# Layer 0's attention: score products and transposes alternate, the projection goes in quarters, the out-projection's weights are fetched in one go

## The chip, the core and the metric

One core of a Trainium2 chip runs the whole program. The metric is the device time of one execution in microseconds (us), as the median of several runs. Beside it there is one execution taken by the hardware profiler. Engines are named as in the profile: PE (TensorE matmul), PEld (its weight load), DVE (VectorE), ACT (ScalarE), POOL (GpSimd), SP (the queue that issues the transfers).

## What is computed

A two-layer block of a transformer over 512 latent tokens and 256 context tokens, width 1024, in float32. Each layer is attention followed by a gated feed-forward network, both with a normalisation and a shift, scale and gate that come from a small conditioning vector. The change touches only the attention of layer 0, which is cut here to what matters:

```python
def _even_mixer(hx, hc, w_in, w_out, ...):      # hx: 512 tokens, hc: 256 tokens
    # 16 query heads of 64 in two groups, A (window, with sink) and B (dense); 4 query heads share one key/value head
    qa, ka, va, qb, kb, vb = split(h @ w_in)    # normalised per head, rotated for latent tokens
    # per head:  s = q k^T / 8 ;  p = softmax(s) ;  o = p v
    # A, latent: keys are the context and a window of 128 on both sides; B, latent: all 768 keys
    # context queries see the 256 context keys only
    out = concat(oa, ob) @ w_out
    x = x + gate * out
```

The four key/value heads give four batches of work, each with four query heads: batches 0 and 1 are A, 2 and 3 are B. The tokens are six tiles of 128: tiles 0 to 3 latent, 4 and 5 context.

## The kernel before

Every float32 product that needs the accuracy is done in two parts, a high and a low one (`hi = cast(x)`, `lo = x - hi`): the cast runs on ACT, the subtraction on DVE or POOL. The helper `unit` (L360 to L371) fetches a block of weights, casts it (L369) and subtracts (L370); its names are `wir`, `wih`, `wil` for the in-projection and `wor`, `woh`, `wol` for the out-projection.

**In-projection** (`in_proj0`, L499). For one batch and one token tile, 24 products `inps` (8 blocks of the contraction, three products each, L465 to L467) add up in one PSUM bank. ACT then copies the bank to `qkv` (L511); DVE rotates, POOL normalises, and the parts `qd` and `kd` are turned on PE (`qpt` L526, `kpt` L534) and copied by ACT to `qt` and `kT`. The turns wait in a list `due` and are taken from it one at a time while later products run. From batch 1 on there is one bank for `inps`.

**Attention** (`attend0`, L538). A step is one batch and one token tile; there are 24 steps in `steps`, in the order of tiles 4, 5, 0, 1, 2, 3 (in batch 3: 0 to 5). For each of its four heads a step forms the scores `sc` on PE (L569, plus mask products L571), then DVE takes the maximum (`mx` or `nm`, L578 to L582), ACT the exponential into `Pt` (L583), and after each pair of heads DVE a reciprocal `rc` (L592) and POOL the scaling of both heads' `Pt` (L595). Then `Pt` is turned by PE (`ppt`, L603, eight products for each two blocks of keys), copied back by ACT (L608) and DVE (L606), and multiplied with the values (`av`, L614). There are two buffers for `sc` and two PSUM banks that `ppt`, `qpt` and `kpt` share.

`scores0(i)` forms the scores of one head of step i, `transposes0(i-1)` turns two key blocks of the step before, `values0(i-1)` forms its `av`. Between them PE gets the next batch's projection in halves of 12 products (`half0`, counts in `HALVES`), and the modulation vectors of later parts (`mod_run`, products `mod` and `modcol`, raw data through a pool of two raw buffers that the weights share).

**What sets the order.** A scheduler orders every engine's instructions; but from the line `manual.__enter__()` on, PE keeps the order in which the program is written. Before the change that begins ahead of the first attention step. The written order of a step in batches 0 to 2 is:

```python
scores0(i); mod_ends(); scores0(i)
half0((n + 1) // 2)
transposes0(i - 1); scores0(i); transposes0(i - 1); scores0(i); transposes0(i - 1)
half0(n // 2)
values0(i - 1)
```

and in the first step of a batch (`elif i`) the four scores and the first two transposes run ahead of both halves. The weights of the next batch are fetched at the first step of a batch, all four units.

**Out-projection** (`OutProj`). Its eight weight units are made by `out_units` in batch 3, two at the end of step 18 (tile 0) and three each at steps 19 and 20, their subtractions turn by turn on POOL and DVE; each raw block waits for one of two raw buffers. The products `ops` (24 for one tile and one half of the width) begin at step 21.

Of the kernel before, what the change touches and what calls it, by code (L numbers as in the profile page):

```python
# [2 lines left out]

# [15 lines left out]
P = 128  # L19
# [43 lines left out]
def backbone(es: ExitStack, tc: tile.TileContext, x, c, ctx, c_ctx, mod_w, mod_b, norm_mix_w, norm_ffn_w,  # L63
# [418 lines left out]
    def weights0(b, wp, subs, new_tile=raw_tile):  # L482
# [3 lines left out]
        ws = []  # L486
        for u in range(4):
# [4 lines left out]
            ws.append(unit(wp, views, [P, 2, 384], WBUF, "wi", subs[u % len(subs)], new_tile))  # L492
        return ws
# [4 lines left out]
    def in_proj0(b, ws, tabs, wp, st, qp, later):  # L498

        wc, tb = tabs[b // 2]  # L500
# [4 lines left out]
        for t in CTX_FIRST:  # L505
            ps = acc_tile("inps", 384, one=0) if b or t in CTX_FIRST[-2:] else p_sc.pool.tile([P, 1024], F32, name="inps", tag="sc", bufs=2)[:, :384]
            project(ps, t, ws, 0, 384, range(4))
            yield
            project(ps, t, ws, 0, 384, range(4, KT))
# [3 lines left out]
            y, r = rotate(raw[:, 0:320], 4, 1, t, wc, tb, wp)  # L513
# [9 lines left out]
            def turn_q(t=t, qd=qd):  # L523
# [3 lines left out]
                qt = qp.tile([P, 4, P], F32R, name="qt", tag="qt", bufs=6)  # L527
# [611 lines left out]
    ws = weights0(0, wp.pool, (nc.vector,), start_tile)  # L1139
# [11 lines left out]
    due = []  # L1151

    proj = in_proj0(0, ws, tabs, wp.pool, even.pool, wp.pool, due)
    state = next(proj)
    for _ in range(2 * NT - 4):
        next(proj)
        if len(due) > 2:
            due.pop(0)()
    o_t = [keep.tile([P, KT, P], F32, name=f"o{t}", tag="xo", bufs=6) for t in range(NT)]
# [20 lines left out]
    def half0(n):  # L1180
        for _ in range(n):
            if len(due) > 2:
                due.pop(0)()
            next(proj, None)

# [11 lines left out]
    manual = tc.manual_schedule(engines={mybir.EngineType.PE})  # L1197
    manual.__enter__()
    HALVES = ((2, 2, 2, 4, 2, 4), (2, 2, 2, 2, 2, 2), (2, 2, 4, 2, 2, 0))
    RUNS = ((0, 0, 1, 1, 1, 0), (0, 1, 1, 1, 1, 1), (0, 0, 0, 1, 1, 1))  # L1200
    if True:
        for i, (b, t) in enumerate(steps):
            j = i % NT
            if j == 0 and b < 3:
                if b == 1:
                    tables0(1, tabs, wp.pool)
                ws = weights0(b + 1, wp.pool, (nc.gpsimd, nc.vector))
            if i == 0:
                for n in range(2):
                    scores0(i)  # L1210
                    scores0(i)
                    half0(1)
            if j == (0 if b else 2) and b < 3:
# [559 lines left out]
```

## Time and profile before

| | |
|---|---|
| median of 3 runs | 1728.89 us (1728.5 to 1729.42) |
| the profiled execution: its time | 1731.22 us |
| its span, first to last instruction | 1729.4 us, so 1.8 us lie around it |
| DVE busy | 1138.0 us, 66% |
| ACT busy | 940.6 us, 54% |
| POOL busy | 695.1 us, 40% |
| bytes read from HBM | 179.91 MB, 111 GB/s with what is written |

A row of the timeline gives the start, the time from the first start to the last end of the merged instructions, engine, line, operation and number; in brackets stands how long the engine sat idle just before it and what released it. The records of `inps` overlap, so that 12 of them lie about 2.1 us apart from start to start where each is shown with 0.34 us. The products `av`, `mod` and `modcol` show two records each. Granted clock is the share of the full TensorE clock that the throttle granted.

### The profile page before, as it was taken

To read this page: it belongs to the slowest core of one execution; us is meant where nothing else is said; L and a number is where in the kernel's file an instruction comes from. 1 tells how busy PE (TensorE), PEld (TensorE's weight loads), DVE (VectorE), ACT (ScalarE), POOL (GpSimd) and SP (SyncE) were. 2 spreads that over 40 slices of the span, in tenths; PEclk is the share of its full clock that TensorE was granted. 3 is DMA by queue.
4 is the path that set the end of the run, shared out by engine and by line. 5 is a ranking of instruction groups with operands and counts; after the bars stand their busy time and mean duration, and the time that the engine had idled before them with its cause. 6 is when DMAs were issued, how large, how long until landed. Compare 5 with 4: busy or idle time off the path is not lost. (4 is left out here: it accounts for less than half of the span.)

```text
span 1729.4 us, 28502 instructions
## 1 busy us (share of the span) xinstructions
PE 1647.4 (95%) x10378; PEld 1481.8 (86%) x10378; DVE 1138.0 (66%) x2009; ACT 940.6 (54%) x2010; POOL 695.1 (40%) x851
## 2 busy tenths in 40 slices
PE   6998989899999999999999899999997999999998
PEld 3877878677999999998777789999986899999887
DVE  3755646554798887767766655666666498887433
ACT  5555556644456655545554456666665465555321
POOL 1655545521345554412413366666643242222000
PEclk8899999999999999999999999999999999999999
DMA  9122221411365555439955311111103153332431
GB/s 315 51 68 67 95 65 50 158 49 50 99 185 164 156 158 167 136 109 342 303 171 163 107 45 62 53 41 44 46 13 122 31 143 103 105 106 58 137 94 69
DMA packets 217964, 194.64 MB, mean 113 GB/s; under 512 B 20000, under 2 KB 202592, under 8 KB 217824
## 3 DMA queue, kind: packets, MB, share of 16 engines
q1 hardware_dynamic: 217472, 192.62, 36.1%
q8 instruction: 81, 1.33, 0.3%
q14 instruction: 59, 0.48, 0.1%
q10 hardware_dynamic: 352, 0.21, 0.0%
HBM read 179.91 MB, written 12.87 MB: 111 GB/s over the span
## 5 line engine op out<-in xcount | busy, mean ns | idle before, releaser
L865 ACT CAST wbh<-wr 128x512 fp32r<-128x512 f32 x170 | 105.3, 621 | 145.5 <-PE p L897 76.5
L897 PE MATMUL p<-hT,wbh 128*128 128x256 f32 (+1 forms) x752 | 154.8, 299 | 0.0
L465 PE MATMUL inps<-wih,hT 128*128 128x384 f32 x384 | 136.7, 356 | 6.1 <-ACT qkv L668 6.0
L467 PE MATMUL inps<-wih,hT 128*128 128x384 f32 x384 | 130.4, 340 | 0.0
L466 PE MATMUL inps<-wil,hT 128*128 128x384 f32 x384 | 130.3, 339 | 0.0
L875 POOL TENSOR_TENSOR wbl<-wr,wbh 128x512 fp32r<-128x512 f32 x43 | 58.0, 1349 | 177.6 <-ACT wbh L865 177.6
L897 PEld LDWEIGHTS p<-hT,wbh 128*128 128x128 f32 x752 | 122.0, 191 | 0.2
L875 DVE TENSOR_TENSOR wbl<-wr,wbh 128x512 fp32r<-128x512 f32 x127 | 106.4, 844 | 22.4 <-ACT wbh L865 18.8
L897 PE MATMUL p<-hT,wbl 128*128 128x256 f32 (+1 forms) x376 | 112.1, 298 | 0.0
L897 PE MATMUL p<-t,wbh 128*128 128x384 f32 (+1 forms) x480 | 111.0, 317 | 0.0
L230 POOL TENSOR_TENSOR modp<-modp 128x512 f32<-128x512 f32 x40 | 57.5, 1439 | 119.1 <-ACT modp L229 119.1
L595 POOL TENSOR_SCALAR Pt<-Pt,rc 128x256 f32<-128x256 f32 (+3 forms) x96 | 74.0, 782 | 75.4 <-DVE rc L592 71.3
L897 PE MATMUL p<-hTt,wbh 128*128 128x256 f32 (+1 forms) x480 | 101.3, 303 | 0.0
L851 POOL TENSOR_TENSOR wr<-wr 128x512 f32<-128x512 f32 x40 | 61.1, 1528 | 88.4 <-DVE ws L856 87.4
L897 PE MATMUL p<-b,wbh 128*128 128x384 f32 x368 | 94.7, 339 | 0.2 <-DVE c L925 0.2
L865 ACT CAST wbh<-ws 128x512 fp32r<-128x512 f32 x120 | 69.5, 580 | 43.4 <-PE p L897 29.5
L370 POOL TENSOR_TENSOR wil<-wir,wih 128x768 fp32r<-128x768 f32 x38 | 71.2, 1874 | 48.6 <-ACT wih L369 48.1
L223 DVE SCALAR_TENSOR_TENSOR ma<-modw,cols,ma 128x256 f32<-128x256 f32 x140 | 85.5, 610 | 2.3
L897 PEld LDWEIGHTS p<-t,wbh 128*128 128x128 f32 x480 | 82.9, 189 | 0.0
L875 DVE TENSOR_TENSOR wbl<-ws,wbh 128x512 fp32r<-128x512 f32 x120 | 81.6, 680 | 1.7 <-ACT wbh L865 1.6
L897 PEld LDWEIGHTS p<-hTt,wbh 128*128 128x128 f32 x480 | 78.4, 191 | 3.1 <-ACT modp L229 2.1
L583 ACT ACTIVATE Pt<-sc,nm 128x256 f32<-128x256 f32 (+3 forms) x96 | 67.6, 706 | 24.6 <-DVE nm L579 15.1
(332 smaller groups left out, 5236.7 us busy)
## 6 DMA issues: line engine op xcount, KB each, us to landing
modw<-in_mod_w_dram SPq DMA_DIRECT2D x96, 512.0 KB, 4.6
wr<-in_ffn_w_in_dram SPq DMA_DIRECT2D x176, 256.0 KB, 3.2
wdr<-in_ffn_w_out_dram SPq DMA_DIRECT2D x66, 512.0 KB, 4.2
wir<-in_od_w_in_dram SPq DMA_DIRECT2D x96, 128.0 KB, 2.3
hidm<-hid SPq DMA_DIRECT2D x44, 192.0 KB, 3.9
hr<-hidm SPq DMA_DIRECT2D x22, 192.0 KB, 3.2
x<-in_x_dram SPq DMA_DIRECT2D x8, 512.0 KB, 8.7
wir<-in_ev_w_in_dram SPq DMA_DIRECT2D x16, 256.0 KB, 2.8
```

Source lines behind the costliest of these rows:

```text
L223: nc.vector.scalar_tensor_tensor(acc, w[:, k], scale[k], acc, ALU.mult, ALU.add)
L230: nc.gpsimd.tensor_add(pr[:, 0:2], pr[:, 0:2], pr[:, 2:4])
L370: (sub or nc.vector).tensor_sub(lo, raw, f32(hi))
L465: nc.tensor.matmul(ps, hs[0][:, k, :], a, start=k == 0, stop=False)
L466: nc.tensor.matmul(ps, hs[0][:, k, :], b, start=False, stop=False)
L467: nc.tensor.matmul(ps, hs[1][:, k, :], a, start=False, stop=k == KT - 1)
L583: turn["exp"] = nc.scalar.activation(p[:, :n], s, AF.Exp, bias=nm[:, c1], accum_out=sm[:, c1])
L595: nc.gpsimd.tensor_scalar(p[:, :n], p[:, :n], rc[:, hh:hh + 1], 1.0, ALU.mult, ALU.mult)
L851: nc.gpsimd.tensor_sub(w, raw[f, "G1"], w)
L865: nc.scalar.copy(hi, w)
L875: (nc.gpsimd if name == "G2" else nc.vector).tensor_sub(lo, raw[need[n]], f32(hi))
L897: nc.tensor.matmul(ps, w[:, k, :], H[b][h][:, k, :], start=first and k == 0 and q == 0, stop=final and k == 3 and q == 2, skip_group_check ...
```

## The change

The PE order of batches 0 to 3 is written anew, and four things around it change.

1. The whole projection of batch 0 is issued before the first attention step (before: 8 of its 12 halves). The first five steps are no longer held to the written order: PE's order there is the scheduler's.
2. The projection goes in quarters of 6 products, `quarters`; a turn from `due` is taken within each pair. In a step of batches 0 to 2 scores and transposes alternate, with a pair of quarters in the middle and one near the end. Every step has the same form, the first one of a batch too. The projection of the next batch starts at its first step in batch 0 as well (before: at the third).
3. Two of a batch's four weight units are fetched two steps ahead of the batch (`j == 4`), with six buffers for each of `wih` and `wil` in place of five.
4. In batch 3 the scores and transposes alternate in the same way.
5. The out-projection's raw weights are fetched by eight transfers in a row into a ring of sixteen blocks and the two raw buffers (`out_units0`); all eight subtractions are on DVE. One unit is made at step 18, two at 19, three at 20, two at 21. In batch 3, and for the first half of tile 3 behind it, the product with the gate goes to a buffer in SBUF and no longer back into PSUM.

```diff
-    for _ in range(2 * NT - 4):
-        next(proj)
...
+    for _ in range(2 * NT):
+        quarters(2)
+        turned0()
...
-    HALVES = ((2, 2, 2, 4, 2, 4), (2, 2, 2, 2, 2, 2), (2, 2, 4, 2, 2, 0))
-    RUNS = ((0, 0, 1, 1, 1, 0), (0, 1, 1, 1, 1, 1), (0, 0, 0, 1, 1, 1))
+    QUARTS = ((((2, 2),) * 6), ((2, 2),) * 6, ((2, 2), (2, 2), (4, 2), (2, 4), (2, 2), (0, 0)))
+    RUNS = ((0, 0, 0, 1, 1, 1), (0, 1, 1, 1, 1, 1), (0, 0, 0, 1, 1, 1))
+    units = weights0(1, wp.pool, (nc.gpsimd, nc.vector))
+    ws = [next(units) for _ in range(2)]
...
+            if i == 5:
+                manual = tc.manual_schedule(engines={mybir.EngineType.PE})
+                manual.__enter__()
...
+            if j == 4 and b < 2:
+                units = weights0(b + 2, wp.pool, (nc.gpsimd, nc.vector))
+                ws = [next(units) for _ in range(2)]
+            if b < 3:
+                n = QUARTS[b][j]
+                scores0(i)
+                mod_ends()
+                transposes0(i - 1)
+                scores0(i)
+                projected(n[0])
+                transposes0(i - 1)
+                scores0(i)
+                scores0(i)
...
+                projected(n[1])
+                transposes0(i - 1)
+                values0(i - 1)
...
+    def out_units0(wp):
+        def tile(name, dtype):
+            return wp.tile([P, D], dtype, name=name, tag="w", bufs=2 * KT)
+
+        raws = [tile("wor", F32) if k < KT - 2 else raw_tile([P, D], "wor") for k in range(KT)]
+        for k, raw in enumerate(raws):
+            nc.sync.dma_start(raw, ev_w_out[0, k * P:(k + 1) * P, :])
+        for raw in raws:
+            hi, lo = tile("woh", F32R), tile("wol", F32R)
+            nc.scalar.copy(hi, raw)
+            nc.vector.tensor_sub(lo, raw, f32(hi))
+            yield hi, lo
...
             if t < 3:
                 with behind("exp"):
-                    ws += [next(units) for _ in range(3)]
-            scores0(i)
-            scores0(i)
...
+                    ws += islice(units, 1)
+                transposes0(i - 1)
+                scores0(i)
+                with behind("exp"):
+                    ws += islice(units, t - 1)
+                transposes0(i - 1)
+                scores0(i)
+                with behind("exp"):
+                    ws += islice(units, 1)
+                scores0(i)
```

The count of every instruction of PE stays the same; of the eight subtractions `wol` of layer 0, four go from POOL to DVE. Where the orders meet the steps of the prediction, they read as follows.

**PE at the first step of batch 2** (tile 4 of the new batch; `av` above it is of batch 1). Before: two heads (`sc` x4 is two products for each of two heads), eight turns, one head, eight turns, one head, and only then the projection.

```order
L614 MATMUL av<-Pt,vv 64x256 x10
L181 MATMUL mod<-modw,s_pad 32x256 x8
L190 MATMUL modcol<-cst,modr 128x2 x2
L287 MATMUL gps<-cst,modc_103 8x128 x2
L569 MATMUL sc<-kT,qt 128x256 x4
L603 MATMUL ppt<-cst,Pt 128x128 x8
L569 MATMUL sc<-kT,qt 128x256 x2
L603 MATMUL ppt<-cst,Pt 128x128 x8
L569 MATMUL sc<-kT,qt 128x256 x2
L526 MATMUL qpt<-identr,qd 128x128 x4
L465 MATMUL inps<-wih,hTc_109 128x384
```

Now:

```order
L613 MATMUL av<-Pt,vv 64x256 x10
L182 MATMUL mod<-modw,s_pad 32x256 x8
L191 MATMUL modcol<-cst,modr 128x2 x2
L288 MATMUL gps<-cst,modc_103 8x128 x2
L568 MATMUL sc<-kT,qt 128x256 x2
L602 MATMUL ppt<-cst,Pt 128x128 x8
L568 MATMUL sc<-kT,qt 128x256 x2
L466 MATMUL inps<-wih,hTc_109 128x384
L467 MATMUL inps<-wil,hTc_109 128x384
```

After the second head stand now two quarters of the projection, 12 products with a turn `qpt` between them, then the second eight turns, the third and fourth head, and two more quarters.

**PE in the middle of batch 0** (the third and fourth head of tile 1 or 2, and the projection of batch 1). Before, in the written order, eight turns, one head with its two mask products, a turn of the query, and the projection:

```order
L603 MATMUL ppt<-cst,Pt 128x128 x8
L569 MATMUL sc<-kT,qt 128x256 x2
L569 MATMUL sc<-kT,qt 128x384 x2
L571 LDWEIGHTS identb
L571 MATMUL sc<-maskb,identb 128x128
L571 LDWEIGHTS identb
L571 MATMUL sc<-maskb,identb 128x128
L526 MATMUL qpt<-identr,qd 128x128 x4
L465 MATMUL inps<-wih,hTc_109 128x384
L466 MATMUL inps<-wil,hTc_109 128x384
```

Now, in the scheduler's order, at the end of the five free steps (the first head of tile 3 stands in the middle):

```order
L602 MATMUL ppt<-cst,Pt 128x128 x4
L613 MATMUL av<-Pt,vv 64x256 x4
L568 MATMUL sc<-kT,qt 128x256 x4
L570 LDWEIGHTS identb
L570 MATMUL sc<-maskb,identb 128x128
L191 MATMUL modcol<-cst,modr 128x2 x2
L602 MATMUL ppt<-cst,Pt 128x128 x4
L533 MATMUL kpt<-identr,kd 128x128 x2
L613 MATMUL av<-Pt,vv 64x256 x2
L602 MATMUL ppt<-cst,Pt 128x128 x4
L613 MATMUL av<-Pt,vv 64x256 x4
```

Five of the six tiles' projections of batch 1 stand further up, among the heads of tiles 4, 5 and 0 and the first of tile 1. From the second head of tile 1 to the second head of tile 3 PE has no projection between the heads.

**DVE in steps 19 and 20 of batch 3** (`nm` is the maximum of one head, `wol` an out-projection unit's subtraction, `hT` the operand of the out-projection). Before:

```order
L582 TENSOR_REDUCE nm<-sc 128x1
L606 COPY Pt<-ppt 128x4x128
L370 TENSOR_TENSOR wol<-wor,woh 128x1024
L592 RECIPROCAL rc<-sm 128x2
L582 TENSOR_REDUCE nm<-sc 128x1 x2
L764 TENSOR_TENSOR hT_108<-o_716,hT_107 128x8x128
L606 COPY Pt<-ppt 128x4x128
L582 TENSOR_REDUCE nm<-sc 128x1
L592 RECIPROCAL rc<-sm 128x2
L370 TENSOR_TENSOR wol<-wor,woh 128x1024
```

Now:

```order
L581 TENSOR_REDUCE nm<-sc 128x1
L605 COPY Pt<-ppt 128x4x128
L760 TENSOR_TENSOR wol<-wor,woh 128x1024
L581 TENSOR_REDUCE nm<-sc 128x1
L605 COPY Pt<-ppt 128x4x128
L581 TENSOR_REDUCE nm<-sc 128x1
L760 TENSOR_TENSOR wol<-wor,woh 128x1024
L591 RECIPROCAL rc<-sm 128x2
L581 TENSOR_REDUCE nm<-sc 128x1
L605 COPY Pt<-ppt 128x4x128
L760 TENSOR_TENSOR wol<-wor,woh 128x1024
L591 RECIPROCAL rc<-sm 128x2
```

Two or three subtractions stand now in one step, the first of them between the turned block of the step before and the maximum of the second head.

More of the change, by code (lines that the diff above doesn't have):

```diff
@@ L2 @@
 from contextlib import ExitStack, contextmanager
+from itertools import islice
 import numpy as np
@@ new lines, in backbone @@
+                proj = in_proj0(b + 1, ws, tabs, wp.pool, (even if b % 2 else odd).pool, due)
+                nxt = next(proj)
+            if j == 4 and b < 2:
[11 more added lines that the diff above has]
+                scores0(i)
+                if j == 0 and b == 1:
+                    tables0(1, tabs, wp.pool)
+                projected(n[1])
+                transposes0(i - 1)
+                values0(i - 1)
```

134 lines of the change are left out of this document (52 added, 82 removed).

## The prediction

> **What bounds the kernel now.** I read the page's line of engines first, then a table of stretches for the stage that changes (42 to 441 us, cut where batches end; its columns are the length, the busy us of PE, PEld, DVE, ACT and POOL, the granted clock, the DMA share and GB/s), then the waits of PE in the same stretches.
>
> ```profile
> PE 1647.4 (95%) x10378; PEld 1481.8 (86%) x10378; DVE 1138.0 (66%) x2009; ACT 940.6 (54%) x2010; POOL 695.1 (40%) x851
> ```
>
> ```profile
> 42.00:67.00 25.00, 23.26 (x124) 21.44 (x116) 19.05 (x39) 11.69 (x24) 12.93 (x17) 0.87 0.26 73
> 67.00:149.30 82.30, 75.86 (x550) 65.44 (x550) 52.66 (x145) 50.12 (x136) 50.16 (x82) 0.98 0.21 63
> 149.30:305.80 156.50, 146.84 (x1074) 121.67 (x1078) 87.52 (x223) 89.81 (x232) 81.80 (x127) 0.97 0.22 67
> 305.80:345.50 39.70, 32.16 (x246) 23.96 (x244) 23.73 (x35) 27.67 (x51) 19.63 (x15) 0.96 0.50 173
> 345.50:441.00 95.50, 93.16 (x490) 73.49 (x489) 45.61 (x81) 45.77 (x92) 21.57 (x30) 1.00 0.16 48
> ```
>
> PE bounds every stretch: no other engine is busy over 70% in the three with attention. The stretches are the projection of batch 0; the rest of batch 0; batches 1 and 2; batch 3 up to the first `ops`; and the out-projection. PE stands still in them for 25.00 − 23.26 = 1.7, 6.4, 9.7, 7.5 and 2.3 us, 27.7 together. Since the change leaves the count of every PE instruction as it is, that sum, and what the clock loses behind it, is all that it can win. The waits, by what ended them, for 42 to 149, 149 to 306 and 306 to 346 us:
>
> ```profile
> PE kpt L534 <- ACT Pt L608: 1.8, 2, 1.1
> PE sc L569 <- ACT kT L535: 1.8, 1, 1.8
> PE inps L465 <- ACT hTc L1134: 1.3, 1, 1.3
> ...
> PE sc L569 <- ACT Pt L583: 5.2, 2, 2.8
> PE kpt L534 <- ACT Pt L608: 2.2, 4, 1.1
> ...
> PE ppt L603 <- ACT Pt L608: 2.8, 1, 2.8
> PE ppt L603 <- POOL Pt L595: 2.7, 4, 1.0
> ```
>
> They are short waits on the softmax chain at places where PE has scores and turns but no projection between them. A long one costs clock as well:
>
> ```profile
> 68.83 1.07 PE L569 MATMUL sc<-kT,qt 128*128 128x256 f32 x4 [1.78 <-ACT kT L535]
> 74.09 0.34 PE L465 MATMUL inps<-wih,hT 128*128 128x384 f32 x1
> 76.21 0.63 PE L569 MATMUL sc<-kT,qt 128*128 128x256 f32 x4
> ...
> 153.14 0.51 PE L569 MATMUL sc<-kT,qt 128*128 128x256 f32 x2 [2.36 <-ACT Pt L583]
> 156.04 0.65 PE L465 MATMUL inps<-wih,hTc 128*128 128x384 f32 x1
> 159.69 0.52 PE L467 MATMUL inps<-wih,hTc 128*128 128x384 f32 x1
> ...
> 232.63 0.60 PE L569 MATMUL sc<-kT,qt 128*128 128x256 f32 x2 [2.81 <-ACT Pt L583]
> 233.03 1.91 PE L603 MATMUL ppt<-cst,Pt 128*128 128x128 f32 x8
> ...
> 338.54 1.88 PE L603 MATMUL ppt<-cst,Pt 128*128 128x128 f32 x8 [2.78 <-ACT Pt L608]
> ```
>
> The rows are single groups with start, duration and, in brackets, the wait ahead. From the first `inps` of twelve to the next scores it is 2.1 us at 74 us (0.18 us each); behind the wait of 2.36 us it is 3.65 us from the first start to the twelfth, 0.33 us each, so 1.8 us more for twelve. I put 1.8 us to that wait, 1.5 to the one of 1.78 us, 0.9 to the one of 2.81 us (eight turns in 1.91 us, against about 1.0) and 1.6 to the one of 2.78 us (1.88, and the next turns too): 5.8 us, in the second, third (2.7) and fourth stretch. In reach are thus 27.7 + 5.8 = 33.5 us.
>
> [...]
>
> **The change part by part.** *The alternating order in batches 1 and 2* (9.7 + 2.7 = 12.4 us in reach). At a batch's first step the third head waited 2.36 and 2.81 us because its buffer was still held by the first head's exponential. Now two quarters (2.1 us) and sixteen turns (twice 0.8 us, by the first two starts below) stand between second and third head, over 4 us in all, and these two waits with their clock go: −7.9 us. The waits of `kpt` for a turn's copy (2.2 us) go too, since turns and `kpt` stand apart. What is late next is the first turn of the step before, which moves ahead of the second head and of two quarters. Its chain:
>
> ```profile
> 190.46 1.04 PE L603 MATMUL ppt<-cst,Pt 128*128 128x128 f32 x8
> 191.26 0.84 PE L569 MATMUL sc<-kT,qt 128*128 128x256 f32 x4
> 192.26 0.82 DVE L578 TENSOR_REDUCE mx<-sc 128x1 f32<-128x640 f32 x1
> 193.46 0.79 ACT L583 ACTIVATE Pt<-sc,nm 128x640 f32<-128x640 f32 x1
> 194.66 0.17 DVE L592 RECIPROCAL rc<-sm 128x2 f32<-128x2 f32 x1
> 195.00 1.99 POOL L595 TENSOR_SCALAR Pt<-Pt,rc 128x640 f32<-128x640 f32 x2 [1.44 <-DVE rc L592]
> 194.49 1.95 PE L614 MATMUL av<-Pt,vv 128*64 128x256 f32 x16
> 196.37 1.07 PE L181 MATMUL mod<-modw,s_pad 128*32 128x256 f32 x16
> ```
>
> The fourth head ends at 192.2, both last heads are scaled at 197.0: 4.8 us. PE's work between them is now two quarters 2.1, `kpt` 0.2, `av` 1.9, `mod` 1.0 and one head 0.8, so 6.0 us: covered. For the context tiles (keys 256) there are `av` of the tile before, half a head and two quarters, 4.1 to 4.5 us: on the edge, four such steps at up to 0.5 us. A turn `qpt` now has only one quarter (1.05 us) before the second turns need its bank, against an ACT copy behind an exponential (0.79 + 0.2): about 0.3 us in each of 12 steps. The last two weight units are issued behind the `mod` of the fifth latent step; landing, cast and POOL subtraction end about when the third quarter needs them, 0 to 1 us at two places. Sum of new waits 2 + 2 to 3.5 + 0.5, 4.9 us in the middle; gain 12.4 − 4.9 = 7.5, from 4 (all of them double) to 11.
>
> *Batch 0 in free order* (6.4 + 1.5 us, and 1.7 us ahead of it). The first scores stand now behind all of tile 3's 24 products (4.2 us), so that the wait of 1.78 us for `kT` and its 1.5 us of clock go. Tile 2's 24 products are set into the wait for the last parts of `hTc` (1.3 us); against that, ACT and DVE have the cast and subtraction of a further weight unit of batch 1 ahead of those last parts, which may delay them by the same. I book 1.5 us, from −0.5 to 2. What is lost is cover: from tile 1's second head to tile 3's second head there is no projection. That is 14 us of PE's own work with seven heads, each ready for its buffer's next user about 2.2 us after its products (0.8 + 0.2 + 1.0 + latencies, by the chain above); with two buffers and turns and `av` between, I find waits of 0.1 to 0.7 us in front of six of them, 1.7 us, and 0.9 us for a `mod` whose raw data come late. With about 1.5 us among tiles 4, 5 and 0, where ACT is the fullest, 4.1 us stay. Gain 7.9 − 4.1 + 1.5 = 5.3, from 0 to 8.
>
> *Batch 3 up to the first `ops`* (7.5 + 1.6 = 9.1 us). POOL's four subtractions, which held up the scaling, go; DVE gets them.
>
> ```profile
> L370 POOL TENSOR_TENSOR wol<-wor,woh x4: 2350/2375/2382, 319.2 to 344.3; 128x1024 fp32r<-128x1024 f32 x4
> L370 DVE TENSOR_TENSOR wol<-wor,woh x4: 1224/1610/1858, 321.0 to 346.3; 128x1024 fp32r<-128x1024 f32 x4
> L595 POOL TENSOR_SCALAR Pt<-Pt,rc x16: 900/906/1932, 301.8 to 348.5; 128x768 f32<-128x768 f32 x16
> L606 DVE COPY Pt<-ppt x12: 671/686/692, 299.9 to 342.9; 128x512 f32<-128x512 f32 x12
> ```
>
> Per step DVE has four maxima (0.9 each), three copies (0.69), and in step 19 two or three, in step 20 three subtractions (1.2 where POOL is still, 1.6 the median) with an operand of 1.2: 9 to 11 us beside 8.4 us of PE (four heads, three times eight turns, `av` 2.8). DVE comes near to being the bound. I followed two steps by these rows: the second head's maximum stands behind copy and subtraction, so the fourth head, which needs that buffer, waits 1.7 us in step 19; the next turns wait 1.2 us for the scaling (maximum, copy, subtraction, reciprocal and two scalings, 5.5 us, against 4.4 us of PE); step 20 has 1.2 us. That makes 20.9 us for steps 19 and 20, which took 24.9. Step 18 wins 1 us (turns of the last keys move up), step 17 loses 0.4 (fourth head). With some clock lost, gain 3.5, from −2 to 7.
>
> A subtraction on DVE can meet the scaling on POOL:
>
> ```profile
> 339.54 2.81 POOL L595 TENSOR_SCALAR Pt<-Pt,rc 128x768 f32<-128x768 f32 x2
> ```
>
> This pair ran beside a subtraction of DVE and took 1.0 us longer than two times the median of 0.906 us. In the new order most scalings follow their reciprocal, which stands behind the subtraction, so I take one or two such meetings, inside the range above. [...]
>
> *The out-projection.* Its weights land earlier than needed, the last two units are subtracted on DVE during the first 18 of 24 products. 2.3 us idle before, 2.3 after, ±1. The gate product through SBUF costs DVE the same two instructions, off the path. Behind the stage nothing is moved, so what is won stays.
>
> **The sum.** 7.5 + 5.3 + 3.5 = 16.3, say 16 us of the profiled execution's 1731.2 (span 1729.4 and 1.8 around it). That execution lies 2.3 us above the median of the runs, 1728.9, as a constant; forecast 1728.9 − 16 = 1713.
>
> **The rivals.** *The gain of batch 3 is eaten by DVE.* For: 9 to 11 us of DVE beside 8.4 of PE, and meetings with POOL. Then batch 3 gives −2 and the rest its lower half: 6 + 4 − 2 = 8, 1721 us. Chance 0.2.
>
> *All waits go.* Every chain fits under its cover: 33.5 less the 2.3 of the out-projection and 4 us that cannot be covered in batch 3, 27 us, 1702. Against it: the edges of 0.3 to 0.5 us found above. Chance 0.1.
>
> *Slower: the uncovered end of batch 0 stalls.* The seven heads without projection wait as the third head of a batch did, 2.36 to 2.81 us and 0.9 to 1.8 us of clock: 7 × 3.6 = 25 us in place of my 2.6, so that 16 becomes −6 and the time 1735. It decides from about 2.1 us of wait for each head on. Against it: the third head in batch 0's rows had ACT's whole exponential chain in front of it with two casts of weights; here turns and `av` lie between most heads. Chance 0.07.
>
> *The waits go, their clock does not come back.* The slow rows may have another cause than the wait ahead of them, since the stretches' clock (0.98, 0.97, 0.96) is below 1.00 all along. Then the 5.8 us stay in the time: 16 − 5.8 = 10, 1719. [...] Chance 0.06.
>
> *The change moves the waits and no more.* The short waits of 0.5 to 1 us turn up at as many new places: the sum of idle stays within 3 us, 1728. For: the free order knows nothing of POOL's real times (1.2 us for five elements). Chance 0.06. The forecast has the rest, 0.51.
>
> **How the numbers follow.** The forecast's own range, from the lower and upper values taken together by halves, is 1706 to 1720. With the first rival's 1721 and its lower bounds, and part of the second, 1704 to 1726 leaves out about 0.2. 0.2% is 3.5 us, about what a measurement of this kernel can tell from no change. Faster by more: forecast, the first two rivals, the clock's, and most of what lies between, 0.87; within: 0.06; slower: 0.07.
>
> **What would show it.** Right: waits of `sc` for the exponential over 2 us gone at both batch ends, and their slow `inps`; no `wol` on POOL; idle of PE some 4 us in batch 0 from the first scores on, 5 in batches 1 and 2, 5 to 6 in batch 3 up to the first `ops`. Wrong: waits of over 1 us in front of several heads of tiles 1 and 2 in batch 0, `inps` waiting for `wil` at a batch's third quarter by over 1 us, or turns in steps 19 and 20 that wait over 2 us.

## The result

The changed kernel takes 1722.1 us (median of 6 runs, 1718.15 to 1723.62), the kernel before 1728.71 us beside it; the ratio is 0.9955 with a 95% interval of 0.9938 to 0.9973. So it is faster, by 4.7 to 10.7 us where 16 were forecast. The profiled execution has a span of 1720.5 us, 8.9 us less than before. Its line of engines on the page:

```profile
PE 1646.0 (96%) x10378; PEld 1475.8 (86%) x10378; DVE 1150.9 (67%) x2013; ACT 938.2 (55%) x2010; POOL 687.4 (40%) x847
```

Below is the table of stretches again, first of before and then of after, now cut at the same instructions in both: from the first `inps` to the last `av` of tile 2 in batch 0, from there to the same `av` in batches 1 and 2, to the first `ops`, to the first product of the feed-forward, and at the end layer 1's attention. Columns are length, busy us of PE, PEld, DVE, ACT and POOL (in brackets the number of instructions), granted clock, DMA share and GB/s.

```profile
43.42:149.24 105.82, 97.64 (x662) 85.94 (x662) 70.27 (x179) 60.51 (x159) 63.03 (x98) 0.96 0.21 62
149.24:225.87 76.63, 71.99 (x544) 60.14 (x548) 44.44 (x128) 42.76 (x120) 39.33 (x68) 0.96 0.24 75
225.87:305.82 79.95, 74.94 (x534) 61.61 (x538) 43.14 (x96) 47.05 (x112) 42.55 (x60) 0.98 0.20 60
305.82:347.00 41.18, 33.64 (x252) 25.28 (x253) 24.47 (x36) 29.14 (x53) 21.11 (x16) 0.96 0.49 166
347.00:441.03 94.03, 91.69 (x482) 72.15 (x480) 44.87 (x81) 44.30 (x90) 20.07 (x29) 1.00 0.16 48
974.44:1378.10 403.66, 378.30 (x2484) 351.73 (x2483) 241.55 (x479) 246.87 (x613) 235.88 (x357) 0.99 0.17 52
```

```profile
42.57:144.02 101.45, 97.53 (x645) 83.36 (x649) 70.91 (x180) 59.90 (x158) 61.95 (x97) 0.97 0.21 60
144.02:222.35 78.33, 73.74 (x564) 61.03 (x568) 48.56 (x130) 44.52 (x123) 41.65 (x69) 0.96 0.31 92
222.35:301.04 78.69, 74.33 (x537) 60.46 (x537) 46.15 (x95) 45.42 (x112) 41.74 (x60) 1.00 0.17 51
301.04:336.91 35.87, 31.61 (x246) 22.96 (x247) 26.92 (x39) 27.09 (x49) 9.77 (x11) 1.00 0.53 191
336.91:430.36 93.45, 91.85 (x481) 71.94 (x480) 46.43 (x82) 47.09 (x94) 21.90 (x30) 1.00 0.18 54
963.57:1369.59 406.02, 378.57 (x2485) 352.11 (x2484) 244.44 (x479) 246.78 (x613) 236.66 (x357) 0.99 0.17 51
```

One run of the modulation (1.5 us of `mod` and `modcol`) lies in batch 0's stretch before and in batch 1's after. With that, batch 0 won 105.8 − 101.4 − 1.5 = 2.9 us, batches 1 and 2 won 156.6 − 157.0 + 1.5 = 1.1 us, batch 3 up to the first `ops` 5.3 us, the out-projection 0.6 us; the first `inps` starts 0.85 us earlier; layer 1's attention, which the change does not touch, lost 2.4 us. That is 8.3 of the 8.9 us; the rest lies in the feed-forwards. So the stage itself won 9.8 us, where the forecast had 16. PE's idle time in it fell from 27.7 to 18.7 us.

The waits of PE answer to those shown of before (2.36, 2.81 and 2.78 us for an exponential or a copy). After the change, in the same stage, and below it in layer 1 before and after (us in total, times, longest):

```profile
199.09 1.12 PE L602 MATMUL ppt<-cst,Pt 128*128 128x128 f32 x4 [2.80 <-ACT qt L527]
319.92 0.97 PE L568 MATMUL sc<-kT,qt 128*128 128x256 f32 x4 [1.59 <-ACT Pt L582]
```

```profile
PE ppt L725 <- DVE hT L772: 2.9, 3, 1.5
```

```profile
PE ppt L724 <- DVE hT L784: 6.7, 3, 5.3
```

The three long waits of before are gone. In their place stands one of 2.80 us, of turns for the copy of `qt`, and one of 5.3 us in layer 1's last step.

### The profile page after: what moved, and what is told of

Its sections match the earlier page's. It is cut to its first block, busy times and chain, and to the rows that moved or that the text cites. A ratio compares the mean times of both kernels' runs of the same rounds, so it can differ in the third digit from the quotient of the medians.

```text
span 1720.5 us, 28519 instructions
## 1 busy us (share of the span) xinstructions
PE 1646.0 (96%) x10378; PEld 1475.8 (86%) x10378; DVE 1150.9 (67%) x2013; ACT 938.2 (55%) x2010; POOL 687.4 (40%) x847
## 5 line engine op out<-in xcount | busy, mean ns | idle before, releaser
L909 PE MATMUL p<-hT,wbh 128*128 128x256 f32 (+1 forms) x752 | 154.8, 299 | 0.0
L909 PE MATMUL p<-hTt,wbh 128*128 128x256 f32 (+1 forms) x480 | 101.3, 303 | 0.0
L466 PEld LDWEIGHTS inps<-wih,hT 128*128 128x128 f32 x384 | 72.8, 190 | 10.7 <-ACT qkv L667 8.5
```

Source lines behind the costliest of these rows:

```text
L466: nc.tensor.matmul(ps, hs[0][:, k, :], a, start=k == 0, stop=False)
L909: nc.tensor.matmul(ps, w[:, k, :], H[b][h][:, k, :], start=first and k == 0 and q == 0, stop=final and k == 3 and q == 2, skip_group_check ...
```

## Two readings of the traces, and two theories

Why did PE wait at the three places before, and at 199.09 us after? ACT's timeline tells it, first of before, then of after:

```profile
149.65 0.83 ACT L369 CAST wih<-wir 128x768 fp32r<-128x768 f32 x1 [1.70 <-DMA wir<-in_ev_w_in_dram]
...
152.52 0.47 ACT L583 ACTIVATE Pt<-sc,nm 128x256 f32<-128x256 f32 x1 [1.28 <-DVE nm L579]
...
230.79 0.83 ACT L369 CAST wih<-wir 128x768 fp32r<-128x768 f32 x1 [2.08 <-DMA wir<-in_ev_w_in_dram]
231.53 0.58 ACT L608 COPY Pt<-ppt 128x512 f32<-128x512 f32 x1
232.00 0.48 ACT L583 ACTIVATE Pt<-sc,nm 128x256 f32<-128x256 f32 x1
...
336.08 1.04 ACT L369 CAST woh<-wor 128x1024 fp32r<-128x1024 f32 x1 [1.85 <-DMA wor<-in_ev_w_out_dram]
337.03 0.90 ACT L583 ACTIVATE Pt<-sc,nm 128x768 f32<-128x768 f32 x1
```

```profile
196.94 0.83 ACT L370 CAST wih<-wir 128x768 fp32r<-128x768 f32 x1 [1.26 <-DMA wir<-in_ev_w_in_dram]
197.68 0.79 ACT L582 ACTIVATE Pt<-sc,nm 128x640 f32<-128x640 f32 x1
198.37 0.19 ACT L582 ACTIVATION_READ_ACCUMULATOR Pt<-sc,nm 128x1 f32 x1
198.46 0.57 ACT L527 CAST qt<-qpt 128x512 fp32r<-128x512 f32 x1
```

The cases are the waits at 153.14, 232.63 and 338.54 us before and at 199.09 us after. In each ACT stands before the cast of a weight block whose transfer hasn't landed, 1.3 to 2.1 us, and the exponential and the copy that PE waits for come behind it in ACT's order. The prediction had seen only PE's row and taken the score buffer for the cause. The buffer was indeed held, but by an exponential that was itself late. The wait of 2.36 us at 153 us has a second part: ACT's cast stood 1.70 us for its transfer there, and its exponential then 1.28 us for DVE's maximum, which came behind four products of the rotation's tables (0.41 us each).

Theory A: the long waits come from what stands ahead of the exponentials on ACT and DVE, above all a cast that stands for its transfer. Theory B, the prediction's: PE's own order makes them, by the score buffers before and by the query's turn with one quarter of cover after.

## The experiments

All stretches are cut as in the tables above; "batches 1+2" is the second and third row together. The ratio is to the kernel before, with its 95% interval. The changed kernel, run a second time, is e12. e11, whose free order mixes the batches, is given in its place below.

| kernel | batch 0 | 1+2 | 3 to `ops` | out-proj. | ratio |
|---|---|---|---|---|---|
| before | 105.8 | 156.6 | 41.2 | 94.0 | 1 |
| after | 101.4 | 157.0 | 35.9 | 93.4 | 0.9955 (0.9938 to 0.9973) |
| e12 after again | 100.9 | 154.2 | 35.9 | 93.4 | 0.9954 (0.9939 to 0.9969) |
| e1 before, casts later | 104.7 | 158.8 | 40.0 | 94.0 | 1.0045 (1.0029 to 1.006) |
| e2 casts later | 112.7 | 160.0 | 35.9 | 93.5 | 1.0042 (1.0025 to 1.0059) |
| e3 weights at the first step | 100.5 | 164.1 | 35.9 | 93.5 | 0.9991 (0.9978 to 1.0005) |
| e4 written order from step 0 | 110.9 | 155.4 | 35.9 | 93.5 | 0.9997 (0.9985 to 1.001) |
| e5 step of before | 101.9 | 156.9 | 36.0 | 93.4 | 0.9964 (0.9949 to 0.9978) |
| e6 batch 3 in the old order | 101.3 | 156.1 | 35.8 | 93.4 | 0.9952 (0.9934 to 0.9969) |
| e7 four subtractions on POOL | 99.9 | 153.5 | 35.9 | 97.4 | 0.9957 (0.9938 to 0.9976) |
| e8 modulation moved | 101.8 | 154.8 | 35.9 | 93.5 | 0.9957 (0.9942 to 0.9973) |
| e9 two raw buffers | 101.5 | 154.1 | 37.2 | 93.4 | 0.9968 (0.9955 to 0.9981) |
| e10, e17 later casts, modulation moved | 99.3, 101.0 | 156.2, 156.3 | 36.0, 35.9 | 93.5, 93.4 | 0.9941 (0.9925 to 0.9957), 0.9959 (0.9946 to 0.9972) |
| e13 all of batch 3 as before | 100.8 | 155.8 | 39.0 | 93.7 | 0.9967 (0.9956 to 0.9978) |
| e14 two buffers, units in lumps | 101.9 | 155.5 | 40.6 | 92.6 | 0.9959 (0.9945 to 0.9972) |
| e15 e5's step, weights at the first step | 102.7 | 162.0 | 35.9 | 93.4 | 0.9985 (0.9972 to 0.9997) |
| e16 two buffers, POOL | 102.5 | 155.8 | 37.2 | 97.8 | 0.999 (0.9974 to 1.0007) |
| e18 e10 with the step of before | 103.0 | 155.9 | 37.3 | 93.4 | 0.9971 (0.996 to 0.9982) |

Where they were not edited, batch 3 and the out-projection repeat to 0.2 us with two exceptions: batch 3 took 37.3 us in e18, and 40.0 us in e1, where the kernel before, with the same batch 3, took 41.2. Batches 1 and 2 took 157.0 and 154.2 us in the changed kernel's two executions; in the 6 us behind their one long wait the granted clock was 0.50 in the first and 1.00 in the second. A stretch stands for one profiled execution of each kernel.

### Who makes the long waits: e1, e2, e8, e10, e17

e1 is the kernel before with only the places of casts and tables moved, and with them the transfers of the last two units (the comments are added here):

```diff
+                    for g in gens[:2]:          # loads at the step's start
+                        next(g)
...
                     scores0(i)
+                    ws += [next(g) for g in gens[:2]]   # casts behind the second head's exponential
```

> The kernel before, its PE order untouched; in the first step of batches 1 and 2 the casts of the new weights stand behind the exponential of the second head and of the fourth, and the tables of the rotation behind the fourth head. Theory A (the long waits at a batch's first step come from what stands ahead of the exponential in the order of ACT and DVE: a cast that waits for its transfer 1.7 to 2.1 us, four table products of 1.6 us): the waits of 2.36 and 2.81 us for the exponential fall under 1 us each and the slow products behind them go, layer 0's attention from its first product to the feed-forward's first takes 393 us or less in place of 397.6. Theory B (the order of PE itself with two score buffers makes them, as the prediction had it): both stay over 2 us, 397 us or more. Layer 1's last step gets the order of the changed kernel on DVE here: if that order costs 2.4 us there, layer 1's attention takes 406 us in place of 403.7.

The waits of `sc` for the exponential at the two batch starts, and the waits of the projection that came instead:

```profile
149.42 0.51 PE L583 MATMUL sc<-kT,qt 128*128 128x256 f32 x2 [0.71 <-ACT Pt L597]
...
228.65 0.51 PE L583 MATMUL sc<-kT,qt 128*128 128x256 f32 x2 [0.71 <-ACT Pt L597]
238.60 0.44 PE L465 MATMUL inps<-wih,hTc 128*128 128x384 f32 x1 [2.03 <-ACT wih L506]
240.49 0.44 PE L466 MATMUL inps<-wil,hTc 128*128 128x384 f32 x1 [1.45 <-POOL wil L507]
```

2.36 and 2.81 us fell to 0.71 each with PE's order untouched, so theory A names the cause. The tables were moved at batch 1's first step alone; for the wait of 2.81 us the casts are enough, and for that of 2.36 us the shares of casts and tables are not separated. But the stage took 397.5 us as before: the weights then arrived late for the projection. Half the expectation failed: removing the cause of a wait won nothing. Layer 1's attention took 407.5 us.

e2 is the changed kernel with the early units' transfers where they were and their casts behind the fourth head's exponential:

```diff
                 scores0(i)
                 scores0(i)
+                if j == 4 and b < 2:
+                    ws = [next(g) for g in gens]
```

> The changed kernel, with the casts of the two early weight units of batches 2 and 3 behind the exponential of the fourth head of the same step, their transfers where they were. Theory A: the wait of 2.8 us of the turns in the fifth step of batch 1 (at 199 us) falls under 0.7 us, layer 0's attention takes 383.5 to 386 us in place of 387.8. Theory B (the turn of a query stands in the turns' bank with one quarter of cover): it stays over 2 us, 387 to 388 us.

The wait for `qt` fell under 0.5 us, but the stage took 402.0 us, 14 more. The waits of PE between 120 and 230 us say why:

```profile
PE mod L182 <- DMA modw<-in_mod_w_dram: 8.0, 4, 4.0
PE ppt L617 <- POOL Pt L609: 2.2, 2, 1.2
```

The weights hold the two raw buffers until their cast and subtraction are done, and the modulation's data go through the same two. In batch 1 it is 14.6 us from the issue of the first transfer to the end of the last subtraction, in place of 8.8, and PE waited 3.3 and 4.0 us for `modw`, a cost that neither theory had.

e8 takes the modulation out of the way instead:

```diff
-    RUNS = ((0, 0, 0, 1, 1, 1), (0, 1, 1, 1, 1, 1), (0, 0, 0, 1, 1, 1))
+    RUNS = ((0, 0, 0, 1, 1, 1), (0, 1, 1, 0, 1, 0), (1, 1, 0, 1, 1, 1))
```

> The changed kernel with two runs of the modulation (mod, modcol) taken out of the fourth and sixth step of batch 1 and put into the first two of batch 2, so that the two raw buffers are free one step earlier for the weights of batch 3, with the same number of instructions. Theory A (ACT stands for the weights' transfer, which stood for a raw buffer that the modulation held): ACT's waits for wir at 194, 197 and 227 us go, the turn's wait of 2.8 us at 199 us falls under 0.7 us, layer 0's attention takes 383.5 to 386 us. Theory B (the query's turn in the turns' bank): the wait stays over 2 us, 387 to 388.5 us.

The stage took 386.0 us. No wait is left at 199 us; the transfers are issued a step's part earlier, the scheduler put the cast earlier too, and the same wait stands there:

```profile
185.89 0.65 PE L602 MATMUL ppt<-cst,Pt 128*128 128x128 f32 x4 [2.40 <-ACT qt L527]
```

```profile
183.74 0.83 ACT L370 CAST wih<-wir 128x768 fp32r<-128x768 f32 x1 [0.95 <-DMA wir<-in_ev_w_in_dram]
184.48 0.79 ACT L582 ACTIVATE Pt<-sc,nm 128x640 f32<-128x640 f32 x1
```

The wait follows the cast, not the step: theory B is out as its cause, and A's hope that an earlier transfer removes it failed as well, since the order gives the cast no more slack than before.

e10 has both, e2's later casts for batch 1's step alone and no modulation in that batch's fifth and sixth step; e17 is e10 once more.

```diff
-    RUNS = ((0, 0, 0, 1, 1, 1), (0, 1, 1, 1, 1, 1), (0, 0, 0, 1, 1, 1))
+    RUNS = ((0, 0, 0, 1, 1, 1), (0, 1, 1, 1, 0, 0), (1, 1, 0, 1, 1, 1))
```

> The changed kernel with the casts of batch 3's two early units behind the fourth head's exponential, and no run of the modulation in the fifth and sixth step of batch 1 (two runs go to the first two steps of batch 2), so that nothing waits for the raw buffers that the later casts hold. Theory A: neither a wait for the query's copy over 1 us nor one for the modulation's transfer is left in batch 1; layer 0's attention takes 382.5 to 385 us in place of 387.8. Theory B (the query's turn): 387 to 388.5 us.

> The kernel of e10_late1 once more. If it is better than the changed kernel, batches 1 and 2 take 155 to 156.5 us again and the ratio to before is again 0.992 to 0.995; if its gain was the lot of the clock behind one wait, the ratio is 0.9945 to 0.997.

No wait for `qt` or `modw` over 1 us is left in batch 1, and the stage took 384.9 and 386.6 us. Yet batches 1 and 2 took 156.2 and 156.3 us, which lies between the changed kernel's two executions (157.0 and 154.2). PE's waits there sum to 8.2 and 8.1 us against 8.4 and 8.0 in the changed kernel's two executions: where one of 2.8 us stood, four of 0.7, 1.4, 0.7 and 1.1 us stand (`av` for `Pt`, turns for POOL's scaling and for `grow`). Behind the 1.4 us PE is slower in e17: from 209.48 to 210.76 us its `inps` stand 0.32 us apart from start to start, from 211.55 us on 0.18 us. The ratio's second value lies on the changed kernel's, so no version here is shown to be better than it.

### The edits one at a time in batches 0 to 2: e3, e4, e5, e11, e15, e18

e3 fetches all four units at a batch's first step:

```diff
-                ws += units
+                ws = ws + list(units) if b == 0 else list(weights0(b + 1, wp.pool, (nc.gpsimd, nc.vector)))
```

> The changed kernel with all four weight units of batches 2 and 3 fetched at the batch's first step, as before the change. Theory A: the wait at 199 us goes, but ACT stands for four transfers ahead of the exponentials at two first steps, and the third quarter's products wait for the last units: 386 to 390 us for layer 0's attention. Theory B: the early fetch has no part in that wait, which stays; with the third quarters' waits of 1 us at two places 389 to 391 us.

```profile
PE inps L467 <- POOL wil L371: 4.5, 4, 1.5
PE inps L466 <- ACT wih L370: 4.3, 2, 2.5
```

Both theories priced it too low: the stage took 393.9 us, batches 1 and 2 took 164.1 us, 7 more. The projection waits 8.8 us for weights.

e4 enters the written order at step 0 (and e11, below, at step 12):

```diff
-            if i == 5:
+            if i == 0:
```

> The changed kernel with the written order of PE from the first step on. If the free order brings what the prediction booked for batch 0 (5.3 us), layer 0's attention takes 391 to 394 us in place of 387.8. If the whole projection ahead of the first scores and the alternation do it and the free order nothing, 386 to 388.5 us.

Batch 0 took 110.9 us, 9.5 more than changed and, with the moved run of the modulation, 6.6 more than before, with waits of 3.63 us for `kd`, 2.40 us for POOL's scaling and 1.40 us for `qt`. The stage took 395.6 us, more than either case had. The free order is worth more than was booked, but most of that only pays for the new written form, which by itself is worse than the old one there.

e5 gives back the step of before from step 5 on (in a batch's first step the projection stands behind all four scores, as before):

```diff
                 scores0(i)
                 mod_ends()
-                transposes0(i - 1)
                 scores0(i)
                 projected(n[0])
                 transposes0(i - 1)
                 scores0(i)
+                transposes0(i - 1)
                 scores0(i)
-                projected(n[1])
                 transposes0(i - 1)
+                projected(n[1])
                 values0(i - 1)
```

> The changed kernel with the step of before (two scores, projection, then turns and scores) from the first written step of batch 0 to the end of batch 2; quarters, early weights and free order stay. Prediction's account (the alternation takes the long waits away, 7.5 us in batches 1 and 2): layer 0's attention takes 392 to 398 us in place of 387.8. Theory A (the early fetch of the weights took them away, the alternation moves short waits only): 386 to 389.5 us, with waits of kpt and qpt for the turns' copies back.

The stage took 388.3 us, batches 1 and 2 156.9: the alternation, on which the prediction had put its largest term, made no difference that can be seen. The wait at 199 us is down to 1.20 us, for another copy, and one of 2.71 us for an exponential stands at the first step of batch 2. ACT stands at both places in the changed kernel too (1.26 us ahead of a cast at 196.94, 1.66 us ahead of one at 227.21), and the order decides which of the two PE feels.

e11 leaves twelve steps to the scheduler:

> The changed kernel with PE in the scheduler's order for the first twelve steps, to the end of batch 1, in place of five. If the free order is better than the written one wherever it stands (7.8 us in batch 0), batch 1 loses its waits of 1.0 and 2.8 us: 383 to 386 us for layer 0's attention. If it was the projection and the late first operands of batch 0 alone that the written order handled badly: 388 to 393 us, with waits of the projection or the turns at new places.

The stage took 389.8 us, 2 more than changed; the ratio is 0.9962 (0.9943 to 0.9981). The free order does not win wherever it stands.

e15 joins e3 and e5:

> The changed kernel with both the step's order of before (from the first written step to the end of batch 2) and the weights fetched at a batch's first step. If the early fetch only pays for the alternation, which asks for the weights half a step earlier: batches 1 and 2 together take 155 to 159 us (157 changed, 156.5 before), though fetching late alone cost 7 us. If the early fetch wins by itself: 161 to 165 us.

162.0 us: the early fetch wins 5 us with the old step as well. But late weights and the old step are what the kernel before had, and it took 158.1 us (with the modulation's 1.5). About 4 us in e15 thus come from something else in the new form, perhaps the quarters or the places of the turns. It is not the clock: in both kernels it stood at 0.50 for 10.2 us of these batches. PE's idle time explains 1.2 us (10.9 against 9.7). The rest stays open.

e18 is e10 with the old step:

> The kernel of e10_late1 with the step's order of before from the first written step to the end of batch 2. If the alternation wins by itself (the prediction's account), batches 1 and 2 take 160 us or more in place of 156.1, with waits of scores for the exponential of over 2 us at a batch's first step. If what counted was that ACT does not stand for a transfer: 154 to 157 us, with the wait of 2.7 us at the first step of batch 2 (e5) gone.

155.9 us, and the wait of 2.7 us is gone: as A expected, the alternation isn't needed. It isn't better either; 1.99 and 1.85 us stand elsewhere. ACT still stands for a transfer in it, 4.50 us ahead of the cast at 209.84, and the 1.99 us of PE, for `qt`, come right behind; the edit did not do all that its expectation supposes.

### Batch 3: e6, e7, e9, e13, e14, e16

The edits undone one by one: e6 the order (two scores ahead of the first turn), e7 the subtractions, e9 the fetch in one go:

```diff
+                scores0(i)                      # e6, and one scores0 less at the step's end
                 transposes0(i - 1)
...
-            nc.vector.tensor_sub(lo, raw, f32(hi))
+            (nc.gpsimd, nc.vector)[k % 2].tensor_sub(lo, raw, f32(hi))      # e7
...
-                units = out_units0(wp.pool)
+                units = out_units(wp.pool, ev_w_out, (nc.vector,))          # e9
```

> The changed kernel with scores and turns of batch 3 in the order of before (steps 18 to 20: two scores, turn, score, turn, score, turn); the out-projection's weights stay as changed. If the alternation brought what was gained there, the stretch from the end of batch 2 to the first product of the out-projection takes 2 to 3 us more: 389.5 to 391 us for layer 0's attention. If the eight transfers in a row and the subtractions on DVE brought it: 387 to 388.5 us.

> The changed kernel with four of the eight out-projection subtractions back on POOL, turn by turn with DVE. If POOL's subtractions held up the scaling (2.35 us each in its queue), the turns of steps 19 and 20 wait 2 to 3 us more: 390 to 391.5 us for layer 0's attention. If it was the late landing of the raw blocks, 387 to 388.5 us, and DVE's relief may even give some tenths back.

> The changed kernel with the out-projection's eight raw blocks fetched through the two raw buffers again, each behind the release of the one before last; order of PE and DVE's subtractions as changed. Theory A (an ACT cast that stands for its transfer holds the exponentials behind it; the eight transfers in a row are what won 5.3 us between the end of batch 2 and the first product of the out-projection): that stretch takes 39 to 41.5 us in place of 35.9, with a wait of PE of over 2 us behind a cast woh that waits for its transfer. Rival (subtractions off POOL, or the order): 36 to 37 us.

To the first `ops` they took 35.8, 35.9 and 37.2 us in place of 35.9. None of them alone is the gain; e7 loses 4.0 us behind it (e16, below, 4.4), where one of the first `ops` waits 3.25 us for a `wol` of POOL, and e9 missed its 39 to 41.5 us though ACT stood 4.0 us for blocks in it. So they were undone together, in e13 all three and the places of the units, in e14 e9's edit and the places, in e16 e9's and e7's:

> The changed kernel with all of batch 3 as before: order of scores and turns, raw blocks through two buffers, subtractions turn by turn on POOL and DVE, two units at step 18 and three each behind the first head of steps 19 and 20. If the 5.3 us between the end of batch 2 and the out-projection come from these edits, the stretch takes 40 to 42 us in place of 35.9, with a wait of turns of over 2 us. If they come from the end of batch 2 (no projection left there), 36 to 37.5 us.

> The changed kernel with raw blocks through two buffers and the units in lumps of two, three and three, subtractions on DVE, order of PE as changed. If a cast that waits for its block stands ahead of the exponentials only where three units follow each other (theory A with the places): 39 to 41 us for that stretch. If ring and places do not matter without POOL's subtractions: 36 to 37.5 us.

> The changed kernel with raw blocks through two buffers and four subtractions on POOL, order of PE and places of the units as changed. A block's buffer comes free only behind POOL's subtraction of 2.35 us there, so the next block lands later. If ring and POOL together made batch 3's waits: 38.5 to 41 us for that stretch; if it takes the lumps too: 36 to 38 us.

e13 took 39.0, e16 37.2, e14 40.6 us. In e14 order and subtractions are the changed kernel's; only the two raw buffers and the places are old:

```diff
                 with behind("exp"):
-                    ws += islice(units, 1)
+                    ws += islice(units, 3)
```

That alone gives 4.7 of the 5.3 us back, as theory A with the places had it; e16, without the lumps, kept to its second case. e13, with more undone, gives only 3.1 back, between its two cases, so the parts do not add up. ACT's waits for the blocks in e14 and in e9, from 295 to 345 us (there is no such row in the changed kernel):

```profile
ACT woh L370 <- DMA wor<-in_ev_w_out_dram: 5.5, 6, 2.8
```

```profile
ACT woh L370 <- DMA wor<-in_ev_w_out_dram: 4.0, 3, 2.7
```

With three units in one place through two buffers ACT stands six times in e14, 0.2 to 2.8 us each, with exponentials behind; spread over the heads (e9) three times, and PE feels little of it. Fetched at once, never. But in e13 and in the kernel before, where the units stand in the same lumps and half of the subtractions are on POOL, ACT stands three times, 4.2 and 2.2 us in all. So e14 shows that lumps through two buffers can cost as much as was won; that they were what cost it before is not shown.

### The changed kernel again: e12

> The changed kernel as it is, beside the others on this chip: 387.8 us again for layer 0's attention if the stretches repeat to some tenths; the wait at 199 us again between 2 and 3 us. Its ratio to before again between 0.994 and 0.997.

384.4 us, not 387.8. Batch 3 and the out-projection repeat to 0.1 us; batch 1 took 75.4 in place of 78.3, with a wait of 2.37 us at the same place and a clock of 1.00 in the 6 us behind it. Layer 1's wait of 5.2 us is there again, and its attention took 405.9 us. The span is 1720.1 us all the same, since layer 0's feed-forward took 535.8 us in place of 533.2; nothing was edited there.

## Why the prediction was wrong, point by point

The sign was right. The stage's sum of waits came near what it said, 18.7 us (the lengths less PE's busy time in the table of after, from the first `inps` to the feed-forward) against about 17, but by errors that offset each other: 9.0 us against 5 in batches 1 and 2, 4.3 against 5 to 6 in batch 3. The gain itself failed by these terms.

- **The alternating order, 7.5 us booked.** This is the step that failed. Batches 1 and 2 won 1.1 us in the one execution and 3.9 in the other, and without the alternation (e5) 1.2. The two waits do go, but their cause was misread: not PE's order with two score buffers, but exponentials that were late behind a cast that stood for its transfer and, at the first of the two, behind products on DVE (e1). The sum also took 2.3 us of short waits as won that it had not named (12.4 less 7.9 and 2.2), and the middle of its new waits is 5.3 us, not 4.9. The early fetch wins 5 to 7 us there (e3, e15) and something in the new form loses most of it. The prediction had the early fetch as a cost of 0 to 1 us at two places.
- **New waits, 4.9 us booked, 8.4 found.** "About 0.3 us in each of 12 steps" for the query's turn was 4.1 us in four, one of 2.8, since that copy stands behind ACT's wait. This is the rival that the waits only move (chance 0.06), in this stretch: whatever was taken away, the sum of waits over 0.15 us, 9.3 us before, stayed at 7.3 to 9.5 us in every version but e1, e2, e3 and e15, which have more.
- **The clock, 5.8 us in reach.** Behind the four waits the clock stood at 0.50 for 17.1 us in all (3.4, 6.8, 3.4 and 3.4), so that they cost up to 8.5 us (an estimate: half of that time). In batch 3 it came back: PE's own time fell from 33.6 to 31.6 us. In batch 1 the new wait took it again (clock 0.50 in the 6 us behind 199.09, 0.96 over the stretch, as before).
- **Batch 0, 5.3 booked, 2.9 found.** Idle fell by 4.3 us (8.2 to 3.9), about as booked. PE's busy time rose by 1.4 us once the moved run is counted, where the clock should have given 1.5 back: the free order breaks turns and `av` from the first scores on into 19 and 11 groups where 10 and 5 stood, and from start to start, where the clock was 1.00, they took 128 and 135 ns each in place of 116 and 119. e4 bears this out: in its written order they stand in 10 and 5 groups and take 118 ns each, and PE's busy time in the stretch, counted with the granted clock, is 91.5 us, against 94.8 in the changed kernel's two executions (before: 93.4, with the moved run's 1.5).
- **Batch 3, 3.5 booked, 5.3 found.** DVE did not become the bound; the rival that had it so (1721 us) has the measured time, but not for its reason. What it owes to the casts' places and landing, which the prediction hadn't counted, e14 makes likely and does not settle; and e1's 40.0 us with the old batch 3 would make the gain 4.1.
- **"Behind the stage nothing is moved", 0 booked.** Layer 1's attention took 406.0 and 405.9 us in the two executions where it took 403.7 (over all versions it varied from 401.9 to 408.9). Its last step has another order on DVE now, the last head's maximum behind a scaling of `e`, and PE waits 5.3 us where it waited 1.5. The scheduler orders the whole program, so an edit in layer 0 can turn an order in layer 1. e1 has that order of DVE too, waits 3.9 us at the same place, and took 407.5 us there. The order was not undone by hand in any run, so its price is read, not tested.

## What to carry to other kernels

When PE waits for an engine, look at what that engine did just before. Here casts that stood 1.3 to 2.1 us for their transfers held up the exponentials and copies behind them, PE waited 2.36 to 2.81 us for these, and moving PE's instructions (e5) only moved the place where that was felt, from 199 us (2.80 us in the changed kernel, 1.20 in e5) to the first step of batch 2 (2.71 us in e5). Spread such casts among the work that depends on the queue, give each transfer a step of lead, and see whose buffer it takes meanwhile. Book a removed wait at what the next late thing leaves of it: here three different cures (the change, e5, e10) left the sum of waits in batches 1 and 2 where it was, 8.0 to 9.5 us against 9.3.

## What the runs showed of the hardware

Behind waits of much the same length the granted clock differed from run to run. The 6 us behind three waits of this stage (after, e5, e12; the columns are those of the tables of stretches):

```profile
199.09:205.09 6.00, 6.00 (x25) 5.29 (x25) 2.77 (x7) 1.42 (x4) 1.77 (x3) 0.50 0.45 141
```

```profile
227.01:233.01 6.00, 6.00 (x45) 4.89 (x45) 2.59 (x6) 3.13 (x9) 2.73 (x5) 1.00 0.56 172
```

```profile
197.78:203.78 6.00, 5.99 (x42) 4.88 (x44) 3.30 (x10) 3.23 (x10) 2.00 (x4) 1.00 0.52 160
```

The waits were 2.80, 2.71 and 2.37 us. Behind the first the clock was 0.50, behind the second and the third 1.00. In e2 it was 0.50 from 219.20 to 225.20 us, behind a wait of only 1.19 us with shorter ones beside it. So the length of a wait alone does not tell in these runs whether it costs clock; what decides it is not shown. The price can be read from batch 1 in the changed kernel and the versions that differ from it in batch 3 alone and have its wait of over 2 us: 75.3 and 75.4 us where the mean clock in the 6 us behind that wait was 1.00 (e9, e12), 76.8 to 77.3 where it was 0.72 to 0.75 (e6, e13, e14, e16), 78.3 where it was 0.50 (after). That is the spread of batch 1 between two executions of one kernel.
